# FFN1 of a hybrid transformer layer: a ring of three pairs of split weights for the down projections, single dots, another first loop

## The chip, the cores and the metric

The kernel runs on one core of a Trainium2 chip. The metric is the device time of one execution in microseconds; the time before is the median of three runs. Five engines work side by side, each through its own queue in order: TensorE (PE; its weight loads are listed as PEld), VectorE (DVE), ScalarE (ACT), GpSimd (POOL), and SyncE (SP), which here only issues transfers.

## The reference

One layer over 512 latent and 256 context tokens of width 1024: a half-step SwiGLU feed-forward network (FFN1), token mixing, and a second one. Each is modulated by nine vectors made from c (latent) and c_ctx (context). The change is in the modulation and in FFN1:

```python
mx = jnp.split((jax.nn.silu(c) @ w_ada + b_ada)[:, None, :], N_MOD, axis=-1)
mc = jnp.split((jax.nn.silu(c_ctx) @ w_ada + b_ada)[None, None, :], N_MOD, axis=-1)
x = ffn_sublayer(x, mx[0], mx[1], mx[2], norm1_w, ffn1_w1, ffn1_w3, ffn1_w2)
ctx = ffn_sublayer(ctx, mc[0], mc[1], mc[2], norm1_w, ffn1_w1, ffn1_w3, ffn1_w2)
...
def swiglu(h, w1, w3, w2):
    return (jax.nn.silu(h @ w1) * (h @ w3)) @ w2
def ffn_sublayer(h_in, shift, scale, gate, norm_w, w1, w3, w2):
    h = modulate(rms_norm(h_in, norm_w), shift, scale)
    return h_in + 0.5 * gate * swiglu(h, w1, w3, w2)
```

Here `modulate(h, shift, scale)` is `h * (1 + scale) + shift`. The inner width is 2816, that is 22 tiles of 128, named f = 0 to 21.

## The kernel before

All values lie with features on the partitions and tokens along the free axis, in the order of two groups A and B of 384 tokens (256 latent and 128 context each). To keep float32 precision with the fp32r matmul, every operand is split in two: a high part (`oph`, a cast on ScalarE, L103) and a low part (`opl`, a subtraction on VectorE, L104). Each product is then three matmuls: high by high (L131), high by low of the right side (L132), low by high (L133). The names in the trace follow: `hh`, `hl` are the halves of the modulated input, `gh`, `gl` those of the gated product, `opl` waits for `oph`.

**Weights.** `Stream.half` (L97) loads 128 x 1024 values into a ring of three buffers (`raw`), `Stream.block` (L89) loads 128 x 2048 into a ring of two (`block`). `operand` (L107) splits 512 columns into a ring of five pairs (`OPS`); up projections, down projections and the weights of later stages take turns in this ring.

**Modulation.** The products of silu(c) and silu(c_ctx) with `w_ada` are made in two ways. `ada_dot` (L225) is a dot on VectorE: a tile of 128 output features by 1024 inputs, times c broadcast over all partitions (`cb`), summed along the row. `ada_row` (L256) makes a row of 2 x 128 on TensorE by eight matmuls, copied by ScalarE, and `ada_col` (L264) turns it into a column by another matmul. In the first loop the scale comes by row, the shift by two dots (`ada_shift`, L270). The other seven vectors come by `ada_half` (L279): one load, and both dots (one from tile 40 on, where only latent tokens need them).

**Start.** Squares of x are made on ScalarE (`square0`), summed by seven adds on VectorE, and one matmul with ones (L423) sums over the partitions. Four warm-up matmuls (L415) stand ahead of it.

**First loop** (L465): over the eight input tiles k, with f = 0 and 1 accumulated in four banks (L462). Step k prepares the input of tile k+1 (`first_x` product, `first_h` shift and cast on ScalarE, `first_l` subtraction), then makes the twelve matmuls of tile k, then the row of tile k+2. The squares of the context are summed by GpSimd (L497) and the context's own matmuls (L455) run some steps later.

**Up projections.** f = 2 and 3 are plain (`up1`). From f = 4 each tile is a Strassen-Winograd pass of seven block products of twelve matmuls (`Winograd`: `head`, `mid`, `tail`), with four banks named X, Y, Z, W. Even tiles take them from the pool of single banks (`mm`), odd tiles from that of double banks (`big`). GpSimd makes the sums of weights (L592, L613 to L615), VectorE those of the results and the gating.

**Down projections.** They run in chunks of 3, 3, 4, 4, 3 and 5 tiles f (`CHUNKS1`), called by `after1` behind f = 5, 6, 10, 14 and 18, and the last after the loop. Each makes 16 sums (`pt`) in single banks, and VectorE adds them, gated, to x (L325).

**Order.** Start and first loop are kept in the order of the program. From L503 on a scheduler orders each engine's queue at build time. `Winograd.run` calls `step` three times per tile, each making one `ada_half`.

Of the kernel before, what the change touches and what calls it, by code (L numbers as in the profile page):

```python
# [16 lines left out]
P = 128  # L17
D = 1024
# [11 lines left out]
NFIRST = 2  # L30
W1 = 2 * NFIRST * P
# [4 lines left out]
WARM = 4  # L36
OPS = 5
GA, GB = (0, 384), (384, 384)
# [43 lines left out]
class Stream:  # L82
# [29 lines left out]
    def halves(self, src, eng=None):  # L112
        o = [self.operand(src[:, i : min(i + 512, src.shape[1])], eng) for i in (0, 512)]
        return Halves([t[0] for t in o]), Halves([t[1] for t in o])

    def unit(self, u, pool=None, tag=None):
        src = self.half(self.dram, u)
        if pool is None:
            return self.halves(src)
# [17 lines left out]
def layer_kernel(ctx: ExitStack, tc: tile.TileContext, xT, wfirst, wst, wada, wuq, wkpe, cols, wrope, vnw, rope, out):  # L137
# [31 lines left out]
    nhalf = const.tile([P, 8], F32, name="nhalf")  # L169

# [43 lines left out]
    units = [first_units(k) for k in range(2)]  # L214
# [41 lines left out]
    def ada_row(r, d):  # L256
        o = pa[0:2, (d % 2) * P : (d % 2) * P + P]
        for kt in range(NK):
            pin(nc.tensor.matmul(o, sc[:, kt, :], r[:, kt * P : kt * P + P], start=kt == 0, stop=kt == NK - 1))
        row = sp.tile([2, P], F32, tag="row", name=f"row_{d}")  # L260
# [3 lines left out]
    def ada_col(row, d):  # L264
        o = pa[:, 256 + 2 * d : 258 + 2 * d]
        pin(nc.tensor.matmul(o, row, ident[0:2, 0:2], start=True, stop=True))
        nc.vector.tensor_scalar(
            pairs[0][1][:, d, :], o, b1[:, NK + d : NK + d + 1], col[:, COL_N1 + d : COL_N1 + d + 1], ALU.add, ALU.mult)

    def ada_shift(r, d, alone=False):  # L270
        for which in range(2):
            ada_dot(r[:, D:], d, which, accs[:, d, which : which + 1])
            if alone:
                nc.vector.tensor_add(mod_s[0][which][:, d : d + 1], accs[:, d, which : which + 1], col[:, d : d + 1])
            yield
        if not alone:
            nc.vector.tensor_scalar_add(pairs[0][0][:, d, :], accs[:, d, :], col[:, d : d + 1])
# [91 lines left out]
    def square0(which, k):  # L369
# [1082 lines left out]
```

## Time and profile before

| | |
|---|---|
| median of three runs | 1205.05 us (1204.18 to 1205.37) |
| the profiled execution: time | 1204.45 us |
| its span, first to last instruction | 1202.7 us |
| its mean granted TensorE clock | 0.986 |
| TensorE busy | 1148.5 us (95%) |
| VectorE busy | 942.0 us (78%) |
| ScalarE busy | 537.1 us (45%) |
| GpSimd busy | 376.1 us (31%) |

The profile is of one execution. A row of the timeline has the start (us from the first instruction), the time of one group, the engine, the line, the operation, the tile written and those read, the shapes and the count; in brackets stands how long the engine was idle before it and what ended that. A line of the waits has the total in us, how often, and the longest. A window has its length, then busy time and count for each engine, the granted TensorE clock, the busy share of the 16 DMA engines and GB/s. L57 is the helper that keeps the start and the first loop in order, so rows there go by the tile's name. A matmul's own time is longer than the step from one to the next, since they overlap.

### The profile page before, as it was taken

The page shows a single profiled execution, that of the slowest core. Times are in us where ns is not written, and L with a number is a line of the kernel's source. Part 1 is how long each engine was busy: PE and PEld are TensorE (multiplying, and loading weights), DVE is VectorE, ACT ScalarE, POOL GpSimd, SP SyncE. Part 2 cuts the span into 40 slices and gives each one's busy share as a digit, 9 for nine tenths or more (in the row PEclk, how much of TensorE's full clock was granted, in tenths as well). Part 3 has the DMA queues.
Part 4 walks back from the last instruction along what each step waited for, and adds up shares of the span by engine and source line. Part 5 has one row for each costly group of instructions (what it writes and reads, how often), then busy time and mean ns, then how long its engine had stood idle before and what let it go on. Part 6 is the DMA issues. An engine that isn't in the chain of part 4 may idle for free. (4 is left out here: it accounts for less than half of the span.)

```text
span 1202.7 us, 18873 instructions
## 1 busy us (share of the span) xinstructions
PE 1148.5 (95%) x7066; PEld 1077.1 (90%) x7066; DVE 942.0 (78%) x1708; ACT 537.1 (45%) x1078; POOL 376.1 (31%) x336
## 2 busy tenths in 40 slices
PE   8899799979999999999999999999899999999998
PEld 6688699979999999999878878898898989899997
DVE  6999997896876877667973878775886878787884
ACT  5463222233144144244553537996553535353451
POOL 1201311222042033024333845784001424243330
PEclk9999999989999999999999999999999999999999
DMA  9444343243623633233322311101113332324212
GB/s 328 162 142 158 108 155 123 94 169 106 214 102 105 207 109 104 67 102 128 109 67 70 109 50 36 37 1 59 48 37 105 106 106 90 122 71 140 105 37 88
DMA packets 35228, 128.53 MB, mean 107 GB/s; under 512 B 3648, under 2 KB 10560, under 8 KB 29504
## 3 DMA queue, kind: packets, MB, share of 16 engines
q1 hardware_dynamic: 34992, 127.25, 31.6%
q8 instruction: 56, 0.92, 0.3%
q14 instruction: 36, 0.29, 0.1%
q10 hardware_dynamic: 144, 0.06, 0.0%
HBM read 125.20 MB, written 2.10 MB: 106 GB/s over the span
## 5 line engine op out<-in xcount | busy, mean ns | idle before, releaser
L103 ACT CAST oph<-block 128x512 fp32r<-128x512 f32 x216 | 134.0, 621 | 243.6 <-PE mm L132 163.9
L104 DVE TENSOR_TENSOR opl<-block,oph 128x512 fp32r<-128x512 f32 x216 | 192.5, 894 | 35.2 <-ACT oph L103 33.8
L131 PE MATMUL mm<-gh,oph 128*128 128x384 f32 (+2 forms) x532 | 187.3, 354 | 4.5 <-DVE x L325 3.9
L133 PE MATMUL mm<-gh,opl 128*128 128x384 f32 (+2 forms) x532 | 186.6, 354 | 4.5 <-DVE opl L104 4.5
L132 PE MATMUL mm<-gl,oph 128*128 128x384 f32 (+2 forms) x532 | 187.5, 352 | 0.0
L103 ACT CAST oph<-raw 128x512 fp32r<-128x512 f32 x140 | 85.5, 619 | 134.4 <-PE mm L132 74.9
L104 DVE TENSOR_TENSOR opl<-raw,oph 128x512 fp32r<-128x512 f32 x140 | 108.0, 778 | 21.6 <-ACT oph L103 21.1
L615 POOL TENSOR_TENSOR block<-block 128x512 f32<-128x512 f32 x35 | 47.2, 1348 | 242.2 <-DVE opl L104 214.5
L592 POOL TENSOR_TENSOR s<-block 128x512 f32<-128x512 f32 x35 | 52.2, 1493 | 216.8 <-DVE g L254 76.1
L131 PEld LDWEIGHTS mm<-gh,oph 128*128 128x128 f32 x532 | 100.1, 188 | 12.3 <-issue 4.3
L133 PEld LDWEIGHTS mm<-gh,opl 128*128 128x128 f32 x532 | 100.2, 188 | 12.0 <-DVE opl L104 5.4
L132 PEld LDWEIGHTS mm<-gl,oph 128*128 128x128 f32 x532 | 100.2, 188 | 6.6
L614 POOL TENSOR_TENSOR block<-s,block 128x512 f32<-128x512 f32 x35 | 51.3, 1467 | 166.7 <-DVE opl L104 165.0
L131 PE MATMUL big<-hh,oph 128*128 128x384 f32 (+1 forms) x240 | 80.1, 334 | 9.6 <-DVE gl L312 7.9
L325 DVE SCALAR_TENSOR_TENSOR x<-mm,g,x 128x256 f32<-128x256 f32 x194 | 71.1, 410 | 13.8 <-PE mm L133 13.7
L132 PE MATMUL big<-hl,oph 128*128 128x384 f32 (+1 forms) x240 | 80.0, 333 | 0.0
L133 PE MATMUL big<-hh,opl 128*128 128x384 f32 (+1 forms) x240 | 79.7, 332 | 0.0
L331 DVE SCALAR_TENSOR_TENSOR x<-mm,g,x 128x512 f32<-128x512 f32 x55 | 41.0, 748 | 48.7 <-PE mm L133 48.7
L229 DVE SCALAR_TENSOR_TENSOR junk<-raw,cb 128x1024 bf16<-128x1024 f32 x48 | 63.2, 1317 | 1.4 <-DMA raw<-wada 1.1
L132 PE MATMUL mm<-hl,oph 128*128 128x384 f32 x160 | 55.0, 344 | 2.5 <-DVE hl L308 2.5
L133 PE MATMUL mm<-hh,opl 128*128 128x384 f32 x160 | 54.4, 340 | 3.2 <-DVE opl L104 3.2
L131 PE MATMUL mm<-hh,oph 128*128 128x384 f32 x160 | 55.0, 343 | 1.1 <-DVE hh L307 0.7
(581 smaller groups left out, 3375.6 us busy)
## 6 DMA issues: line engine op xcount, KB each, us to landing
raw<-wst SPq DMA_DIRECT2D x82, 512.0 KB, 3.8
block<-wst SPq DMA_DIRECT2D x36, 1024.0 KB, 4.9
raw<-wada SPq DMA_DIRECT2D x56, 512.0 KB, 4.1
block<-wada SPq DMA_DIRECT2D x8, 1024.0 KB, 6.6
x<-xT SPq DMA_DIRECT2D x6, 512.0 KB, 6.7
raw<-wfirst SPq DMA_DIRECT2D x8, 256.0 KB, 5.1
out<-x SPq DMA_DIRECT2D x7, 256.0 KB, 2.5
raw<-wuq SPq DMA_DIRECT2D x2, 384.0 KB, 3.0
```

The source lines that it names most:

```text
L103: self.pin(self.nc.scalar.copy(dst[0], src))
L104: self.pin((eng or self.nc.vector).tensor_sub(dst[1], src, dst[0].bitcast(F32)))
L131: nc.tensor.matmul(out, lh, rh, start=first, stop=False, skip_group_check=more)
L132: nc.tensor.matmul(out, lh, rl, start=False, stop=False, skip_group_check=more)
L133: nc.tensor.matmul(out, ll, rh, start=False, stop=last, skip_group_check=more)
L229: nc.vector.scalar_tensor_tensor(out, raw, 1.0, cb[:, which, :], ALU.mult, ALU.mult, accum_out=acc[which][:, c : c + 1] if to is None else to,
L325: nc.vector.scalar_tensor_tensor(x[:, dt, s0 : s0 + sn], pt[:, o : o + sn], mod_g[i][which][:, dt : dt + 1], x[:, dt, s0 : s0 + sn], ALU.m ...
L331: nc.vector.scalar_tensor_tensor(lat(x, dt), two(pt), mod_g[i][0][:, dt : dt + 1], lat(x, dt), ALU.mult, ALU.add)
L592: (eng or nc.gpsimd).tensor_add(s1, q[2], q[3])
L614: eng.tensor_sub(q[0], s1, q[0])
L615: eng.tensor_sub(q[1], q[1], q[0])
```

## The change

FFN1's down projections split their weights into a ring of their own, three pairs in a new pool. In the Winograd passes the modulation is made dot by dot, in steps of 1, 2 and 1 a tile. Even tiles take the single banks in the order X, Y, W, Z. The first block is loaded in two transfers. The sum of squares at the start is four accumulated matmuls over pairs, with two of the squares made on VectorE; the warm-up matmuls go. For tiles 1, 2 and 3 the shift comes with the scale in a row of 256 on TensorE (`ROWS2`; the first blocks of `wada` are packed for it on the host). ScalarE takes over the small scale and shift operations, VectorE the context's squares from GpSimd. The row of tile k+2 now stands between the two halves of step k's matmuls, ahead of the preparation of tile k+1, and the context's part begins a step later.

```diff
+ROWS2 = (1, 2, 3)
-WARM = 4
+DOWNS = 3
...
-    def operand(self, src, eng=None):
-        o = [self.op_pool.tile([P, 512], F32R, tag=f"op{p}", bufs=self.op_bufs, name=f"op{p}_{self.nc.next_id()}") for p in "hl"]
+    def operand(self, src, eng=None, ring=None):
+        pool, tag, bufs = ring or (self.op_pool, "op", self.op_bufs)
+        o = [pool.tile([P, 512], F32R, tag=f"{tag}{p}", bufs=bufs, name=f"{tag}{p}_{self.nc.next_id()}") for p in "hl"]
...
-    units = [first_units(k) for k in range(2)]
+    u0, rw0 = st.raw_pool.tile([P, 2048], F32, tag="block", bufs=BLOCKS, name="block_first"), st.raw()
+    nc.sync.dma_start(u0[:, :D], wada[0][:, :D])
+    nc.sync.dma_start(u0[:, D:], wada[0][:, D:])
+    nc.sync.dma_start(rw0[:, :W1], wfirst[0])
+    units = [(u0, rw0), first_units(1)]
...
     def ada_row(r, d):
-        o = pa[0:2, (d % 2) * P : (d % 2) * P + P]
+        n = 2 * P if d in ROWS2 else P
+        o = pa[0:2, :n]
         for kt in range(NK):
-            pin(nc.tensor.matmul(o, sc[:, kt, :], r[:, kt * P : kt * P + P], start=kt == 0, stop=kt == NK - 1))
+            pin(nc.tensor.matmul(o, sc[:, kt, :], r[:, kt * n : kt * n + n], start=kt == 0, stop=kt == NK - 1))
...
     def ada_col(row, d):
-        o = pa[:, 256 + 2 * d : 258 + 2 * d]
-        pin(nc.tensor.matmul(o, row, ident[0:2, 0:2], start=True, stop=True))
-        nc.vector.tensor_scalar(
-            pairs[0][1][:, d, :], o, b1[:, NK + d : NK + d + 1], col[:, COL_N1 + d : COL_N1 + d + 1], ALU.add, ALU.mult)
+        o = [pcol[:, 4 * d + 2 * i : 4 * d + 2 * i + 2] for i in range(2)]
+        for i in range(2 if d in ROWS2 else 1):
+            pin(nc.tensor.matmul(o[i], row[:, i * P : i * P + P], ident[0:2, 0:2], start=True, stop=True))
+        nc.scalar.activation(
+            pairs[0][1][:, d, :], o[0], AF.Identity, bias=b1n[:, d : d + 1], scale=col[:, COL_N1 + d : COL_N1 + d + 1])
+        if d in ROWS2:
+            nc.scalar.activation(pairs[0][0][:, d, :], o[1], AF.Identity, bias=col[:, d : d + 1])
...
-    def ada_half(i):
-        r = st.half(wada, i)
-        for which in (0, 1) if i < 5 * NK else (0,):
-            ada_dot(r, i, which)
-            if i % NK == NK - 1:
-                mod_final(i // NK, slice(0, NK), which)
+    def ada_rest():
+        for i in range(2 * NK, 9 * NK):
+            r = st.half(wada, i)
+            for which in (0, 1) if i < 5 * NK else (0,):
+                ada_dot(r, i, which)
+                if i % NK == NK - 1:
+                    mod_final(i // NK, slice(0, NK), which)
+                yield
...
-    for i in range(WARM):
-        pin(nc.tensor.matmul(two(warm[:, :256]), ones, ones2, start=True, stop=True))
-    sa = None
-    for k in range(NK):
-        sa = add_sq(sa, k, square0(0, k), nc.vector)
+    for k in range(0, NK, 2):
+        sa = square0(0, k)
+        sb = square0(0, k + 1, k in (2, 6))
+        nc.vector.tensor_add(sa, sa, sb)
+        pin(nc.tensor.matmul(sumx, ones, sa, start=k == 0, stop=k == NK - 2))
...
-    ctx_h = {2: (0, 1), 3: (2, 3), 4: (4,), 5: (5,), 6: (6, 7)}
+    ctx_h = {3: (0, 1), 4: (2, 3), 5: (4, 5), 6: (6, 7)}
+    sqx = {0: 3, 1: 6, 2: 8}
...
+        for i in range(NFIRST):
+            first_mm(k, i)
+        if k + 1 < NK:
+            ada_col(row, k + 1)
+        if later:
+            o = ada_row(units[k + 2][0], k + 2)
+        for i in range(NFIRST, 2 * NFIRST):
+            first_mm(k, i)
         shift = ada_shift(units[k + 2][0], k + 2) if later else iter(())
+        next(shift, None)
         if k + 1 < NK:
             first_x(k + 1, 0)
             ops[k + 1] = st.operand(units[k + 1][1][:, :W1])
             first_h(k + 1, 0)
             next(shift, None)
             first_l(k + 1, 0)
+        if later:
+            row = ada_copy(o, k + 2)
...
-        if k == 0:
-            for j in range(NK):
-                sx = add_sq(sx, j, square0(1, j), nc.gpsimd)
+        if k in sqx:
+            while len(sqs) < sqx[k]:
+                sqs.append(square0(1, len(sqs)))
+                if len(sqs) > 1:
+                    nc.vector.tensor_add(sqs[0], sqs[0], sqs[-1])
...
-            banks = [bigs4[i] for i in (0, 2, 1, 3)] if f % 2 else [mm() for _ in range(4)]
+            mms = None if f % 2 else [mm() for _ in range(4)]
+            banks = [bigs4[i] for i in (0, 2, 1, 3)] if f % 2 else [mms[i] for i in (0, 1, 3, 2)]
...
     def after1(f):
         if f < NPLAIN1:
-            for _ in range(4):
-                ada_step()
+            ada_step(8)
         for ci, n in enumerate(CHUNKS1[:-1]):
             if f == (5 if ci == 0 else (starts1[ci] + n + 1) // 2 * 2):
-                down(starts1[ci], n, U_DN1 + starts1[ci], [GA, GB], lambda pt, dt, g, gn: evac_x(pt, dt, seg_of(g // 384), 0))
+                down(starts1[ci], n, U_DN1 + starts1[ci], [GA, GB], lambda pt, dt, g, gn: evac_x(pt, dt, seg_of(g // 384), 0),
+                     ring=(dnp, "dn", DOWNS))
...
+            dnp = fctx.enter_context(tc.tile_pool(name="ffn1d", bufs=DOWNS))
...
-    Winograd(gp, 384, U_UP1, blocks, g_tile, 1).run(NPLAIN1, after1, ada_step)
+    Winograd(gp, 384, U_UP1, blocks, g_tile, 1).run(NPLAIN1, after1, lambda f, i: ada_step(1 + (i == 1)))
```

More of the change, by code (lines that the diff above doesn't have):

```diff
@@ L435, in layer_kernel @@
     first_l(0, 0)
+    row = ada_copy(ada_row(units[1][0], 1), 1)
     put_cb(1)
@@ L438, in layer_kernel @@
         pass
-    row = ada_row(units[1][0], 1)
-    for _ in ada_shift(units[1][0], 1):
-        pass
-    ada_col(row, 1)
     pbs = bigs(4)
     pcs = []
-    sx = None
     def first_ctx(k):
@@ L482, in layer_kernel @@
             first_h(j, 1)
-        for i in range(2 * NFIRST):
-            first_mm(k, i)
-        if later:
-            row = ada_row(units[k + 2][0], k + 2)
-        next(shift, None)
         for j in ctx_h.get(k, ()):
@@ L491, in layer_kernel @@
             first_ctx(j)
-        next(shift, None)
-        if later:
-            ada_col(row, k + 2)
-        if k == 0:
-            for j in range(NK):
-                sx = add_sq(sx, j, square0(1, j), nc.gpsimd)
-        if k == 1:
+        if k in sqx:
[3 more added lines that the diff above has]
+                    nc.vector.tensor_add(sqs[0], sqs[0], sqs[-1])
+        if k == 2:
             sumx = mm()[:, :256]
-            pin(nc.tensor.matmul(sumx, ones, sx, start=True, stop=True))
+            pin(nc.tensor.matmul(sumx, ones, sqs[0], start=True, stop=True))
         if k == 5:
```

78 lines of the change are left out of this document (41 added, 37 removed).

## The prediction

> **What bounds the kernel now.** I read the page first (busy shares), then the waits of TensorE in the first half, then the busy times by stage, then the timeline at each long wait.
>
> ```profile
> PE 1148.5 (95%) x7066; PEld 1077.1 (90%) x7066; DVE 942.0 (78%) x1708; ACT 537.1 (45%) x1078; POOL 376.1 (31%) x336
> ```
>
> TensorE is busy 1148.5 of 1202.7 us. So a gain can only come from its 54 us of idle time, or from time at a lowered clock. The waits of TensorE up to 620 us (total, times, longest) say what the idle time is:
>
> ```profile
> PE mm L133 <- DVE opl L104: 9.3, 5, 3.2
> PE big L131 <- DVE gl L312: 7.9, 1, 7.9
> PE mm L500 <- POOL sq L57: 3.9, 1, 3.9
> PE big L131 <- DVE sl L319: 1.1, 2, 0.9
> PE big L131 <- ACT p L605: 0.6, 1, 0.6
> PE mm L131 <- ACT oph L103: 0.6, 1, 0.6
> PE big L131 <- ACT oph L103: 0.6, 1, 0.6
> ```
>
> The long ones are waits for VectorE, and one for GpSimd. The stages (us; busy time and count of PE, weight loads, DVE, ACT, POOL; granted clock; DMA share; GB/s):
>
> ```profile
> 0.00:20.49 20.49, 16.27 (x85) 12.54 (x85) 11.44 (x23) 13.11 (x22) 0.68 (x6) 1.00 0.97 325
> 20.49:78.03 57.54, 50.18 (x292) 38.78 (x292) 54.38 (x107) 31.22 (x68) 8.88 (x7) 0.97 0.57 196
> 78.03:150.86 72.83, 62.19 (x349) 59.44 (x350) 71.56 (x114) 25.04 (x50) 17.66 (x11) 0.99 0.38 125
> 150.86:156.11 5.25, 5.25 (x16) 5.25 (x17) 5.25 (x10) 0.96 (x2) 0.00 (x0) 0.50 0.91 357
> 248.00:262.00 14.00, 6.11 (x22) 5.79 (x21) 14.00 (x26) 3.32 (x7) 4.12 (x3) 0.63 0.63 228
> 262.00:484.00 222.00, 222.00 (x1280) 221.68 (x1278) 172.22 (x308) 75.54 (x141) 55.58 (x39) 1.00 0.41 136
> ```
>
> From 20 to 151 us VectorE is busy 126 of 130 us and TensorE waits 18 us: this stretch is bound by VectorE. The same holds at 248 us for one long wait. From 262 to 484 us TensorE never waits; there nothing can be won. The stages after FFN1 are not touched.
>
> **Part 1: the start (0 to 20.49 us).** The squares of x were summed on VectorE in one chain of seven adds, then one matmul. Now two squares are made on VectorE, pairs are added (six operations), and four matmuls accumulate.
>
> ```profile
> 7.13 5.47 DVE L57 TENSOR_TENSOR sq<-sq,sq 128x512 f32<-128x512 f32 x7 [2.68 <-ACT sq L57]
> 10.48 1.89 PE L415 MATMUL mm<-ones 128*128 128x256 f32 x8
> 12.66 1.12 PE L423 MATMUL mm<-sq,ones 128*128 128x512 f32 x2 [0.29 <-DVE sq L57]
> 20.18 0.38 PE L266 MATMUL mm<-ident,row 2*128 2x2 f32 x2 [1.34 <-ACT row L57]
> 20.49 0.50 PE L462 MATMUL big<-hh,oph 128*128 128x512 f32 x1
> ```
>
> Seven dependent adds took 5.47 us, 0.78 each; six that wait less take about 0.72 each, 4.3. So the last add ends 1.2 us earlier, and the three earlier matmuls lie under it. The first main matmul then waited at 20.18 for a row copied on ScalarE behind the second big copy of c (L436); in the new order that copy comes after the row's. Against it stands the doubled row of tile 1 (+1.7, below). The first block now comes in two transfers, one more issue on SP's queue ahead of block 1 and of the context's x; the queues behind it are full at this time, so it costs nothing beyond the place in the queue. I take 1.8 us gained, between 0.5 and 2.5.
>
> The four warm-up matmuls of L415 leave. The Trainium skill (TensorE: Matmul & The Clock Gate, Part 1) says that the array falls to half clock after an idle window of about 3.4 us, which speaks against taking them out: the first 3.4 us of work would then cost 1.7 us more. Without them the gap would be 10.5 to 12.7, 2.2 us, and the earlier matmuls of the squares lie in it; by the trace I expect no loss, by the rule at its worst 1.7 us.
>
> **Part 2: the first loop (20.49 to 78.03 us).** Work leaves VectorE:
>
> ```profile
> L57 DVE SCALAR_TENSOR_TENSOR junk<-block,cb 128x1024 bf16<-128x1024 f32 x15 | 19.3, 1289 | 0.2 <-ACT cb L57 0.2
> L57 DVE TENSOR_TENSOR hl<-hfull,hh 128x256 fp32r<-128x256 f32 x7 | 2.8, 419 | 0.0
> L57 DVE TENSOR_SCALAR s<-accs,col 128x2 f32<-128x2 f32 x7 | 2.3, 325 | 0.1
> L57 DVE TENSOR_SCALAR a<-mm,b,col 128x2 f32<-128x2 f32 x7 | 1.9, 275 | 2.4 <-PE mm L266 2.4
> 27.23 9.35 POOL L57 TENSOR_TENSOR sq<-sq,sq 128x256 f32<-128x256 f32 x7 [25.95 <-ACT sq L57]
> 26.62 0.69 DVE L57 TENSOR_TENSOR hl<-hfull,hh 128x512 fp32r<-128x512 f32 x1
> 33.15 1.20 DVE L57 TENSOR_TENSOR hl<-hfull,hh 128x512 fp32r<-128x512 f32 x1
> ```
>
> Six dots go (tiles 1 to 3 get their shift from TensorE): 6 x 1.14 (start to start, rows in part 4) = 6.8. The small scale and shift operations go to ScalarE (31 of 57.5 us busy): 2.3 + 1.9 = 4.2. GpSimd's seven adds go; while they ran (9.35 us) the same VectorE subtraction took 1.20 instead of 0.69, so about 3 us more. Seven adds of 256 columns come, at 0.42: 2.9. Net 11 us off 54.4: VectorE needs 43 us and is no longer the bound.
>
> TensorE becomes it. Its rows of the modulation cost:
>
> ```profile
> 20.49:78.03 57.54, 11.45 (x96) 7.65 (x96) 18.89 (x30) 0.00 (x0) 0.00 (x0) 0.97 0.57 196
> ```
>
> Six rows in 11.45 us, 1.91 each, with 128 columns. Three are now 256 wide. The doubling costs between nothing (fixed cost) and 1.9; the 16 records follow each other at about 0.11 us, so it is the columns that count, and I take 1.7. Two of the three lie in this loop: +3.4, and +0.5 for three more column matmuls. TensorE's work at full clock is 50.18 less 1.7 (half of the 3.4 us at half clock that 0.97 of 57.54 makes) = 48.5, so 52.4 now. To this I add 2 us for two waits that I see in the new order: tile 2's row now stands in the middle of step 0, and its block comes over queues that are 97% busy at 325 GB/s (x of 768 columns, 3.1 MB, three blocks of 1.05 and two first weights of 0.26 are 6.8 MB: 21 us, against 20 when TensorE asks); and the sum of the context's squares ends on VectorE just as TensorE wants it. So 54.5 against 57.54: 3 us, between -2 and 5.
>
> A wait is added: VectorE's product with x (L390) now waits for ScalarE's scale, and behind it in VectorE's queue stand the split of the weights and the subtraction hl, for which TensorE's next step waits. From the column matmul it is ScalarE, VectorE, twice ScalarE, VectorE, some 0.7 each as hl above and 0.3 for the first: 3.1 us. TensorE has the next tile's row (1.9 or 3.6) and half a step of products (six at 0.23) in that time, 3.3 or more, and the context's products from step 4: covered, but with little to spare in step 3, which is why my lower bound is below zero.
>
> **Part 3: up to the first down projection (78.03 to 156 us).** TensorE idles 72.83 - 62.19 = 10.6 us, and its last wait costs clock as well:
>
> ```profile
> 150.86 0.69 PE L133 MATMUL mm<-gh,opl 128*128 128x384 f32 x1 [3.18 <-DVE opl L104]
> 151.35 0.52 PE L131 MATMUL mm<-gh,oph 128*128 128x384 f32 x1
> 151.67 0.52 PE L132 MATMUL mm<-gl,oph 128*128 128x384 f32 x1
> 156.81 0.33 PE L132 MATMUL mm<-gl,oph 128*128 128x384 f32 x1
> 156.98 0.33 PE L133 MATMUL mm<-gh,opl 128*128 128x384 f32 x1
> ```
>
> Matmuls start 0.32 us apart until 156.1 and 0.17 after: 5.25 us at half clock, 2.6 lost. Up to the tile f=5 the built program now has 24 dots after the first loop where there were 35, since dots come one by one instead of in pairs: 11 x 1.14 = 12.5 us off VectorE's 71.6, so 59 against TensorE's 62.2, and it arrives with a lead from the loop as well. The waits that are not backlog (ScalarE's copies and the gating product, 1.1 + 0.6 + 0.6 + 0.6) stay: 2.9. Gain 10.6 - 2.9 + 2.6 = 10.3, between 5 and 13. The ring itself (down weights no longer take turns with the up weights' five buffers) is in this term: the wait at 150.86 is for a down weight. At each turn of the new ring ScalarE waits for TensorE to let go of a pair, as it does now.
>
> **Part 4: the long wait (248 to 262 us).**
>
> ```profile
> 242.48 1.28 DVE L104 TENSOR_TENSOR opl<-block,oph 128x512 fp32r<-128x512 f32 x2
> 243.69 1.21 DVE L229 SCALAR_TENSOR_TENSOR junk<-raw,cb 128x1024 bf16<-128x1024 f32 x1
> 244.83 2.31 DVE L229 SCALAR_TENSOR_TENSOR raw<-raw,cb 128x1024 f32<-128x1024 f32 x1
> 249.28 0.56 DVE L637 TENSOR_TENSOR big<-big,u 128x384 f32<-128x384 f32 x1
> 249.75 0.55 DVE L634 TENSOR_TENSOR big<-big,sl 128x384 f32<-128x384 f32 x1
> 256.46 0.69 PE L131 MATMUL big<-hh,oph 128*128 128x384 f32 x1 [7.89 <-DVE gl L312]
> 261.42 0.53 PE L131 MATMUL mm<-u4h,oph 128*128 128x384 f32 x1
> 262.16 0.34 PE L131 MATMUL mm<-u4h,oph 128*128 128x384 f32 x1
> ```
>
> By start to start a dot costs 1.14 us (beside GpSimd up to 2.3), a split 0.6, a 384-wide operation 0.47. The pass up to f=8 held 8 dots: 8 x 1.14 + 8 x 0.6 + 8 x 0.47 = 17.7, and more beside GpSimd, against 84 matmuls x 0.173 = 14.5 on TensorE. Now the passes f=8 to 10 hold 4, 4 and 3 dots: 4.6 + 4.2 + 3.8 = 12.6, about 15 with GpSimd. The backlog that made the wait (7.9, and matmuls of 0.53 instead of 0.34 from 256.5 to 261.7 behind it, 2.6 us) grows by half a microsecond a pass instead of 3 to 6. Gain 9.5, between 4 and 10.5. The new bank order (W before Z in even tiles) helps the same release and is not counted again.
>
> **Part 5: the rest.** The dots go somewhere: the down projections behind f=10 and f=14 hold 15 where there were 12, which is 3.4 us of VectorE in stretches of 48 us of TensorE, hidden while VectorE (172 of 222 us) has room. A dot that waits for its load has the evacuations of x behind it, and those free the four banks of the down projection. I charge 1 us, from 0 to 6, and 1 us more for the new turns of the ring.
>
> **The sum.** The profiled execution took 1204.45 us (span 1202.7, and 1.75 around it); the median of the runs is 1205.05, so no correction. 1.8 + 3 + 10.3 + 9.5 - 2 = 22.6: 1204.45 - 22.6 = 1182.
>
> **Rivals.** *The loop gives nothing*: TensorE's 5 us of wider rows and their waits for blocks eat what VectorE gives up. For it: queues at 97%. Against: from block 3 on a step of 6 us needs 1.3 MB, 4 us at 325 GB/s. Parts 3 to 5 alone: 1187.
>
> *A wait comes back later*: VectorE falls behind in a pass that held no dots before (f=12, 16, 17), or behind a late load, once for as long as the wait at 248: 7.9 + 2.6. For it: every dot moved is moved to a later place. Against: 50 us of room from 262 to 484. 1193.
>
> *The change doesn't do what it says*: the backlog is of splits and GpSimd's slowing rather than dots, so parts 3 and 4 give a third: 1182 + 13 = 1195.
>
> *Slower*: ScalarE stands at the cast of a down pair until TensorE lets go of one of only three, and behind it wait the casts of the next up products. 22 units in two pairs are 44 turns. For it: casts already held TensorE 0.6 us at a time. From 0.55 us a turn it eats the 24.6 us that the other parts bring, at 0.7 with two falls to half clock (5 us) the time is 1204.45 + 11 = 1216. Against: five shared buffers made just one long wait in a down projection so far.
>
> **How the numbers follow.** Forecast 0.55; loop nothing 0.17; wait back 0.12; backlog of splits 0.07; slower 0.09. The forecast's own range is 1176 to 1190. The range is 1174 (all parts at their upper bounds, less a little) to 1198 (the third rival with a small loss). Faster than 0.2% (2.4 us, about what a measurement can tell from no change): the first three and most of the fourth, 0.87; same 0.04; slower 0.09.
>
> **What would show it.** The first main matmul near 18.7 us; the wait on GpSimd's squares gone; VectorE near 43 us busy in the first loop; no 3.18 and 7.89 waits and no half clock at 151 and 256; the product that waited until 150.86 near 138. I am wrong if a wait of over 3 us stands anywhere from 80 to 480 us, or if ScalarE's waits for TensorE at down weights stop TensorE.

## The result, and the profile after

The changed kernel is slower by 0.55%: 1208.48 us (median of 7) against 1202.33 of the kernel before on the same chip, ratio 1.0055 [1.0039, 1.0071]. The profiled execution has a span of 1205.1 us against 1202.7, so the two profiles lie closer together than the medians. First the busy times of its page, then TensorE's waits up to 620 us (total, times, longest):

```profile
PE 1151.6 (96%) x7070; PEld 1072.5 (89%) x7070; DVE 931.9 (77%) x1686; ACT 539.5 (45%) x1093; POOL 365.8 (30%) x329
```

```profile
PE big L133 <- DVE u L638: 17.7, 4, 7.3
PE mm L133 <- DVE hh L324: 1.8, 2, 1.1
PE big L472 <- DVE hl L58: 1.8, 2, 1.1
PE mm L135 <- DVE opl L105: 1.8, 3, 1.1
```

The waits of 7.9, 9.3 and 3.9 us (for `gl`, `opl` and GpSimd's `sq`) are gone. In their place stands one kind that the kernel before did not have: 17.7 us for the Y sum, the addition of bank Y and the copied first product (`u`, L638). The windows by stage (busy time and count for PE, weight loads, DVE, ACT, POOL; granted clock; DMA share; GB/s):

```profile
0.00:18.73 18.73, 16.64 (x81) 9.63 (x81) 10.09 (x20) 10.97 (x19) 0.68 (x6) 1.00 0.97 319
18.73:78.33 59.60, 53.47 (x300) 38.21 (x300) 45.38 (x87) 36.82 (x85) 0.00 (x0) 1.00 0.55 201
78.33:150.35 72.02, 63.25 (x357) 61.01 (x357) 71.40 (x114) 26.32 (x53) 17.34 (x11) 1.00 0.41 133
248.00:262.00 14.00, 12.20 (x69) 11.57 (x68) 14.00 (x22) 6.75 (x13) 4.99 (x3) 1.00 0.31 88
324.00:339.00 15.00, 7.67 (x37) 7.35 (x36) 10.86 (x23) 3.38 (x6) 1.60 (x2) 0.77 0.80 287
425.00:438.00 13.00, 7.37 (x27) 7.06 (x26) 11.46 (x22) 2.86 (x5) 1.94 (x2) 0.74 0.89 310
```

The first window ends with the first main matmul, the second with the first plain product (78.03 before). In the stretch at 248 us TensorE is busy 12.20 of 14 us now (6.11 before); the holes are at 332 and 431, at the ends of the down projections behind f=10 and f=14. From TensorE's timeline:

```profile
150.35 0.44 PE L133 MATMUL big<-u3h,oph 128*128 128x384 f32 x1 [3.98 <-DVE u L638]
332.20 0.69 PE L133 MATMUL big<-u3h,oph 128*128 128x384 f32 x1 [7.33 <-DVE u L638]
...
431.54 0.69 PE L133 MATMUL big<-u3h,oph 128*128 128x384 f32 x1 [5.63 <-DVE u L638]
```

A mark along the way is the start of the Y sum of each tile on VectorE (after minus before, us; negative is earlier):

| f | 5 | 6 | 7 | 8 | 9 | 10 | 11 | 14 | 15 | 16 | 17 | 21 |
|---|---|---|---|---|---|---|---|---|---|---|---|---|
| after | -0.98 | -2.57 | -4.29 | -11.01 | -11.07 | -9.64 | -3.12 | -2.19 | +5.18 | +7.49 | +8.89 | +7.44 |

So 11 us are won up to f=9 and 18.5 lost from there to f=21, in two steps of 6.5 and 7.4 us, each with a down projection in it, and smaller ones. What stands in VectorE's queue at the first of them, the changed kernel first, then the kernel before:

```profile
328.70 1.23 DVE L236 SCALAR_TENSOR_TENSOR raw<-raw,cb 128x1024 f32<-128x1024 f32 x1 [0.92 <-DMA raw<-wada]
329.85 0.08 DVE L236 DVE_READ_ACCUMULATOR raw<-raw,cb 128x1 f32 x1
329.85 0.69 DVE L105 TENSOR_TENSOR opl<-block,oph 128x512 fp32r<-128x512 f32 x1
330.45 1.22 DVE L236 SCALAR_TENSOR_TENSOR raw<-raw,cb 128x1024 f32<-128x1024 f32 x1
331.60 0.08 DVE L236 DVE_READ_ACCUMULATOR raw<-raw,cb 128x1 f32 x1
331.60 0.55 DVE L638 TENSOR_TENSOR u<-big,p 128x384 f32<-128x384 f32 x1
```

```profile
329.14 1.22 DVE L229 SCALAR_TENSOR_TENSOR raw<-raw,cb 128x1024 f32<-128x1024 f32 x1
...
331.62 1.39 DVE L325 SCALAR_TENSOR_TENSOR x<-mm,g,x 128x256 f32<-128x256 f32 x4
332.92 1.89 DVE L104 TENSOR_TENSOR opl<-block,oph 128x512 fp32r<-128x512 f32 x3
334.72 0.55 DVE L620 TENSOR_TENSOR u<-big,p 128x384 f32<-128x384 f32 x1
```

After, the last dots stand behind the last x additions and directly ahead of the Y sum, each paced by its load, and TensorE's W product, in the same double bank as Y, waits 7.33 us. Before, the last dot ended at 330.4 with x additions and splits still to come, and TensorE never waited. The loads and casts show what has changed ahead of the dots (SyncE's and ScalarE's timelines and the first product of the down projection; after, then before):

```profile
276.33 0.44 PE L133 MATMUL mm<-gh,dnh 128*128 128x384 f32 x1 [0.33 <-ACT sl L635]
306.01 0.62 ACT L104 CAST dnh<-raw 128x512 fp32r<-128x512 f32 x1 [3.53 <-PE mm L134]
289.66 37.74 SPq L100 DMA_DIRECT2D raw<-wada  x14
331.70 6.77 SPq L100 DMA_DIRECT2D raw<-wst  x3
336.17 1.14 ACT L104 CAST dnh<-raw 128x512 fp32r<-128x512 f32 x2 [3.46 <-DMA raw<-wst]
```

```profile
290.24 0.34 PE L131 MATMUL mm<-gh,oph 128*128 128x384 f32 x1
307.00 0.62 ACT L103 CAST oph<-raw 128x512 fp32r<-128x512 f32 x1 [3.55 <-PE mm L132]
295.87 28.99 SPq L99 DMA_DIRECT2D raw<-wada  x12
```

A down weight keeps its load buffer until its second half is cast. With three pairs the last such cast comes 29.7 us after the first product, with five it came at 16.8; meanwhile the dots have fewer of the three buffers. (Some products run ahead in the changed kernel. Counted back from the last product, at 318.30 and 328.08, the cast is 12.3 and 21.1 us away: 9 us later, not 13.) And the pairs that fall free at the end are taken at once by the next chunk: its casts (336.17) stand in ScalarE's queue 41 us ahead of that chunk's first product (377.54), and wait for loads that SyncE issues behind the dots' (331.70).

### The profile page after: what moved, and what is told of

It reads as the page before. It is cut to its first block, busy times and chain, and to the rows that moved or that the text cites. A ratio compares the mean times of both kernels' runs of the same rounds, so it can differ in the third digit from the quotient of the medians.

```text
span 1205.1 us, 18833 instructions
## 1 busy us (share of the span) xinstructions
PE 1151.6 (96%) x7070; PEld 1072.5 (89%) x7070; DVE 931.9 (77%) x1686; ACT 539.5 (45%) x1093; POOL 365.8 (30%) x329
## 5 line engine op out<-in xcount | busy, mean ns | idle before, releaser
L133 PE MATMUL mm<-gh,dnh 128*128 128x384 f32 x352 | 118.1, 336 | 0.6 <-ACT sl L635 0.3
L134 PE MATMUL mm<-gl,dnh 128*128 128x384 f32 x352 | 117.8, 335 | 0.0
L135 PE MATMUL mm<-gh,dnl 128*128 128x384 f32 x352 | 116.9, 335 | 0.8 <-DVE dnl L105 0.7
L104 ACT CAST oph<-raw 128x512 fp32r<-128x512 f32 x86 | 52.4, 620 | 58.9 <-PE mm L134 31.4
L105 DVE TENSOR_TENSOR opl<-raw,oph 128x512 fp32r<-128x512 f32 x86 | 64.2, 754 | 10.9 <-ACT oph L104 10.7
L134 PE MATMUL mm<-gl,oph 128*128 128x512 f32 (+1 forms) x180 | 69.3, 385 | 0.0
L135 PE MATMUL mm<-gh,opl 128*128 128x512 f32 (+1 forms) x180 | 69.1, 385 | 0.0
L133 PE MATMUL mm<-gh,oph 128*128 128x512 f32 (+1 forms) x180 | 68.8, 385 | 0.0
L133 PEld LDWEIGHTS mm<-gh,dnh 128*128 128x128 f32 x352 | 66.2, 188 | 1.8 <-ACT dnh L104 1.0
L135 PEld LDWEIGHTS mm<-gh,dnl 128*128 128x128 f32 x352 | 66.0, 188 | 1.5 <-DVE dnl L105 1.5
```

The lines of the kernel that those rows point to most:

```text
L104: self.pin(self.nc.scalar.copy(dst[0], src))
L105: self.pin((eng or self.nc.vector).tensor_sub(dst[1], src, dst[0].bitcast(F32)))
L133: nc.tensor.matmul(out, lh, rh, start=first, stop=False, skip_group_check=more)
L134: nc.tensor.matmul(out, lh, rl, start=False, stop=False, skip_group_check=more)
L135: nc.tensor.matmul(out, ll, rh, start=False, stop=last, skip_group_check=more)
```

## The experiments

Eighteen kernels; "before" is the kernel before in the same session. The last column names the expectation (given below, ahead of each result) in whose range the time lies.

| run | kernel | us | ratio to before | in the range of |
|---|---|---|---|---|
| e1 | changed, dots in pairs | 1219.01 | 1.0144 [1.0123, 1.0164] | B |
| e2 | changed, no ring | 1199.58 | 0.9984 [0.9972, 0.9996] | none, between A and B |
| e3 | before, with the new start and first loop | 1201.12 | 0.9987 [0.9976, 0.9998] | none, nearest to "gives nothing" |
| e4 | changed, five dots a tile to f=9, then three | 1223.11 | 1.0169 [1.0147, 1.0190] | B |
| e5 | e1, next chunk's loads held | 1206.48 | 1.0032 [1.0016, 1.0048] | none, 2.5 above O |
| e6 | changed, next chunk's loads held | 1208.77 | 1.0055 [1.0037, 1.0074] | T |
| e7 | changed, eight pairs in one ring | 1203.08 | 1.0010 [0.9996, 1.0024] | none, between O and M |
| e8 | no ring, two load buffers for the dots | 1214.16 | 1.0107 [1.0073, 1.0142] | the rival |
| e9 | no ring, dots held | 1216.67 | 1.0101 [1.0079, 1.0123] | G |
| e10 | changed, dots held | 1207.64 | 1.0046 [1.0027, 1.0065] | O |
| e11 | changed, ring of two pairs | 1213.24 | 1.0076 [1.0052, 1.0100] | D |
| e12 | changed, dots and loads held | 1209.55 | 1.0056 [1.0038, 1.0073] | D |
| e13 | no ring, three lots of 12 dots | 1207.11 | 1.0023 [1.0012, 1.0034] | none |
| e14 | no ring, lots of 13 and 14 | 1202.75 | 0.9998 [0.9984, 1.0011] | W |
| e15 | ring, three lots of 12 between the sums | 1197.37 | 0.9935 [0.9918, 0.9952] | none, 0.6 below D |
| e16 | e15, lots behind the sums | 1210.71 | 1.0063 [1.0041, 1.0085] | none, 0.7 above P |
| e17 | e15, lots two sums later | 1193.87 | 0.9908 [0.9884, 0.9933] | none, 0.1 below P |
| e18 | e15, next chunk's loads held | 1203.92 | 1.0008 [0.9990, 1.0026] | none |

**One part at a time (e1 to e4).** Theory A: the dots in the down projections are too many and their loads late. Theory B: the ring does it. e1, dots in pairs:

```diff
-                yield
+            yield
...
-            ada_step(8)
+            ada_step(4)
...
-lambda f, i: ada_step(1 + (i == 1))
+lambda f, i: ada_step()
```

> The changed kernel with one part undone: the modulation dots in pairs again, three loads a tile as before (12 dots behind f=10 and f=14 instead of 15 to 16). Theory A (too many loaded dots behind a down projection's end): the waits of 7.3 us at 332 and 5.6 us at 431 and the half clock behind both go, about 20 us; the passes up to f=9 hold 8 dots again, so up to 10.5 us come back near 248: between 1190 and 1199 us. Theory B (the ring of three pairs makes those waits): they stay, and the time is 1208 or above.

e2, no ring (both calls of `down`):

```diff
-            dnp = fctx.enter_context(tc.tile_pool(name="ffn1d", bufs=DOWNS))
...
-                     ring=(dnp, "dn", DOWNS))
```

> The changed kernel without the second ring: down weights share the five pairs again, dots stay single. Theory A: 13 and 16 dots stand behind f=10 and f=14, 3 and 2 of them behind the last addition to x, so waits of 3 to 6 us stay near 330 and 430: 1203 to 1210 us. Theory B: both waits go and the time falls by 15 us or more, to 1193 or less.

e3 has the edits of e1 and e2, and the old order of banks:

```diff
-            mms = None if f % 2 else [mm() for _ in range(4)]
-            banks = [bigs4[i] for i in (0, 2, 1, 3)] if f % 2 else [mms[i] for i in (0, 1, 3, 2)]
+            banks = [bigs4[i] for i in (0, 2, 1, 3)] if f % 2 else [mm() for _ in range(4)]
```

> The kernel before with the new start and first loop alone (dots in pairs, no second ring, old bank order). If the loop is worth what was forecast, 1197 us (5 less than before). If it gives nothing, because TensorE's wider rows eat VectorE's relief (first plain product at 78.3 us against 78.0), within 1 us of before, with the waits at 151 and 248 as they were.

e4, another pace of the dots:

```diff
-lambda f, i: ada_step(1 + (i == 1))
+lambda f, i: ada_step((2 if i else 1) if f < 10 else 1)
```

> The changed kernel with another pace of the dots: five a tile up to f=9, three a tile from f=10, so that 12 dots stand behind f=10 and f=14 as before. Theory A: neither the waits at 332 and 431 nor the long one at 248 (5 dots a pass instead of 8): 1186 to 1194 us, below both kernels. Theory B: the waits at 332 and 431 stay, 1203 us or more.

The ring costs 8.9 us with single dots (1208.48 against e2, from two sessions) and 17.9 with pairs (e1 against e3, which also differ in the banks). The loop and the start give 1.3 us. In e1 the long wait is still there (7.91 us, at 255.51), so the new order of banks does not remove it; the single dots do. In e2 the waits near 330 and 430 fall to 2.77 us or less, but its Y sum, 12.3 us ahead of the kernel before at f=9, is only 1.9 ahead at f=21: the single dots lose 10.4 us there without any ring (e3, with pairs, loses nothing there). In e4 12 dots stand in each of the two down projections, as before, and it is the slowest of all: A falls as a theory of the count. In e1 and e4 the long waits behind the two down projections are not at the Y sum but at a cast (6.07 and 3.78 us; 5.77 and 5.73 us). ScalarE's and TensorE's timelines of e1 show how:

```profile
337.19 1.14 ACT L104 CAST dnh<-raw 128x512 fp32r<-128x512 f32 x2 [7.48 <-DMA raw<-wst]
338.23 0.61 ACT L104 CAST oph<-block 128x512 fp32r<-128x512 f32 x1
...
341.39 0.61 ACT L104 CAST oph<-block 128x512 fp32r<-128x512 f32 x1
```

```profile
341.54 0.69 PE L133 MATMUL mm<-hh,oph 128*128 128x384 f32 x1 [6.07 <-ACT oph L104]
```

The casts of the chunk behind f=14 wait 7.48 us for their loads, the casts of tile f=11 wait behind them, and TensorE behind those.

**The next chunk's casts, and the memory (e5 to e8).** e5 (on e1) and e6 (on the changed kernel) tie the loads of a chunk's first two units to its last gated product, by a copy of one column:

```diff
-    def half(self, src, i):
+    def half(self, src, i, late=None):
         t = self.raw()
+        if late is not None:
+            self.nc.gpsimd.tensor_copy(t[:, :1], late)
...
-                        us[q] = st.unit(u0 + q, ring=ring)
+                        us[q] = st.unit(u0 + q, ring=ring, late=gt[f0 + n - 1][0][:, :1].bitcast(F32) if ring and cache is None and q in (0, 1) else None)
```

> Changed kernel with dots in pairs (as in the run that took 1219.01), ring kept, but the loads of a chunk's first two down units are held until the chunk's last gated product exists (a one-column GpSimd copy into the load's buffer). Theory O (order): the ring's cost is that its pairs are free as soon as a down projection ends, so the casts of the NEXT chunk are put there, ahead of the casts of the up pass that follows, and stand in ScalarE's queue for late loads (7.48 us at 337 in that run). Then this run has no wait over 3 us at the up product behind f=10 and f=14, and takes 1199 to 1204. Rival T (turns): three pairs are too few, a cast stands until TensorE lets go of one. The turns are the same here, so 1214 to 1221.

> The changed kernel itself with the same hold. Theory O: the casts of the next chunk leave the passes f=11 and f=15, and the time falls to that of the kernel without the ring (1199.6), 1196 to 1201; of the waits of 7.33 and 5.63 us at the Y sum behind f=10 and f=14 at most 3 us each stay, since 15 dots paced by loads are still there. Rival T: as the changed kernel, 1206 to 1210.

e7, the same pairs in one ring, and e8, the memory for load buffers instead:

```diff
+        self.turn = (self.turn + 1) % (self.op_bufs + DOWNS)
+        ring = self.more if self.turn < DOWNS else None
```

```diff
-            r = st.half(wada, i)
+            r = adp.tile([P, 1024], F32, tag="adaraw", bufs=DOWNS, name=f"adaraw_{i}")
+            nc.sync.dma_start(r, wada[i // 2][:, (i % 2) * 1024 : (i % 2) * 1024 + 1024])
```

> The changed kernel with the same eight pairs in one ring, in which up and down weights take turns. Theory O: turns in program order keep the next chunk's casts out of the pass that follows, so 1195 to 1201 although the memory is the same. Rival M (any more pairs let the splits run ahead of the sums and dots on VectorE, whichever ring): no better than the changed kernel, 1206 or more.

> No second ring; the dots' loads get two buffers of their own instead (8 KB a partition where the ring took 12). Theory O says further that what singles gain up to f=9 (12.3 us in the run without the ring) is given back where 13 to 16 dots paced by loads through three shared buffers stand in a down projection. Here 10 and 8 are there, and 5 to 6 in each of the passes between, so the 12.3 us are kept: 1188 to 1193. Rival: five to six dots a pass are more than VectorE has room for (6 x 1.14 + 7 x 0.6 + 8 x 0.47 = 14.8 us against 14.5 of TensorE) and the wait moves there: 1198 or more.

With pairs the hold gives back 12.5 of 17.9 us, and no wait over 3 us is left behind f=10 and f=14: there the early casts are the larger part of the ring's cost. In the changed kernel it gives nothing (e6: 5.67 and 5.49 us of waits at the Y sum remain, behind dots). So the early casts are not its bound; the time is in T's range, but the waits end with VectorE's Y sum and not with a cast, so T's reason is not shown by it. e7 lies between the two bounds. e8 missed by over 20 us: with buffers of their own the dots run ahead to where VectorE has no room. The Y sum of f=4 comes 9.7 us later than before, and from f=11 to f=14, with five or six dots a pass, another 15 us go.

**The dots held (e9 to e12).** From f=11 each dot's load is tied in the same way to the gated product of the tile before, so that 4 to 8 stand in a down projection; e9 without the ring, e10 with it, e12 with the hold of e6 as well. e11 changes `DOWNS` alone.

```diff
-            r = st.half(wada, i)
+            r = st.half(wada, i, late[0])
...
+    def paced(f, i):
+        late[0] = gt[f - 1][0][:, :1].bitcast(F32) if f >= 11 else None
+        ada_step(1 + (i == 1))
```

```diff
-DOWNS = 3
+DOWNS = 2
```

> No second ring, and from f=11 the load of a dot waits for the gated product of the tile before (a one-column GpSimd copy into its buffer), so that dots cannot be pulled into a down projection: 4, 8 and 8 stand behind f=10, 14, 18 instead of 13, 16 and 4, and 3 to 5 in the passes between. Theory D (crowding): the 12.3 us that single dots gain up to f=9 were given back because 13 to 16 loads of 2.4 us each through three shared buffers do not fit into a down projection of 39 us, and VectorE works in order. Then 1188 to 1193, faster than both kernels. Rival G: the extra GpSimd copies, or dots in passes that had none, cost as much: 1197 or more.

> The changed kernel with its ring, dots held in the same way (4, 5 and 4 behind f=10, 14, 18). Theory D: with three pairs a down weight sits in its load buffer until its last half is cast, 27.5 us into the down projection instead of 16.8, so the dots' loads start late, and the last dot ends 48 to 51 us after the start instead of 40. That hurts through the dots alone, so here the ring costs little: no wait over 3 us from 280 to 450, 1189 to 1196. Rival O (the casts of the next chunk, put ahead of the next pass, do the harm by themselves): 1200 or more.

> The changed kernel with a ring of two pairs instead of three. Theory D: the last cast of a down unit comes one turn of 4.15 us later still (30 us or more into the down projection), the last dot too, so 1209 to 1218. Rival O (casts of the next chunk put ahead): one pair less can be put ahead, so less harm: 1200 to 1206.

> The changed kernel with its ring, and both the dots' loads (as in the run before last) and the first two down loads of a chunk held. Theory D: as the run with held dots and ring, within 3 us of it, since without crowded dots the early casts find their loads in time. Rival O: at least 5 us better than that run.

In e10 the wait behind f=10 is gone (Y sum of f=11 at -11.3 us against before, -3.1 in the changed kernel): dots at the end of a down projection are what TensorE waited for. But the gain is lost again: by f=14 it is -3.3, for eight dots in the passes f=13 and 14. So e10 missed D, and its time lies in the range of Rival O; but e12, which takes the early casts away as well, is no better than e10, which speaks against O. e11 did what D said (last cast 33.0 us after the first product, waits of 5.26 and 5.96 us). e9 missed D by over 20 us. Two things follow: fewer pairs do not help (e11's interval overlaps that of the changed kernel, so that they make it worse is not shown), and from f=11 on the dots have no cheap place in the passes.

**The dots dealt out between the sums (e13 to e18).** Four dots a tile up to f=10, then one behind each of the first twelve of a down projection's 16 sums, held as in e9. e13 is without the ring, e15 with it; e14 is e13 with thirteen and no dots at f=10.

```diff
+    def evac_dot(pt, dt, g, gn):
+        evac_x(pt, dt, seg_of(g // 384), 0)
+        if left[0] > 0 and (2 * dt + (g > 0)) >= 0 and (2 * dt + (g > 0)) % 1 == 0:
+            left[0] -= 1
+            ada_step()
...
+        if f in (10, 14, 18):
+            left[0], late[0] = 12, gt[f - 1][0][:, :1].bitcast(F32)
```

> No second ring; single dots, four a tile up to f=10 as in the change, and the rest in three lots of 12 dealt out between the sums of the down projections behind f=10, 14 and 18 (each load waits for the gated product of the tile before), none in the passes between. Theory D: twelve loads of 2.4 us fit into a down projection (the kernel before does it, last dot 40 us after the start), so the 10 to 12 us that singles gain up to f=10 are kept to the end: 1189 to 1194. Rival W (VectorE's whole work up to f=21 sets the pace, wherever the dots stand): 1198 to 1203, as without the ring.

> The same with no dots at f=10 and 13, 13 and 14 in the three lots. Theory D: the wait behind f=9 (2.1 to 2.3 us for a cast at 260 in the runs without the ring) shrinks, the last dot of a lot ends 2.4 us later, about 42 us after the start of the down projection and still before the next Y sum at 44: within 2 us of the run before, 1188 to 1195. Rival W: 1198 to 1203.

> The changed kernel with its ring and the same three lots of 12. Theory D: the down weights sit in the load buffers until 27.5 us into the down projection instead of 16.8, so the last dots end some 8 us later than in the run without the ring, at 46 to 48 us, past the next Y sum, and the ring costs 3 to 6 us at each of three places: 1198 to 1208. Rival N (the ring is harmless once the lots are right): within 3 us of the run with twelve and no ring.

e16 puts the lots behind the sums, e17 lets them begin two sums later, e18 adds the hold of e6 to e15:

```diff
-            ada_step()
...
+                ada_step(left[0])
+                left[0] = 0
```

```diff
-        if left[0] > 0 and (2 * dt + (g > 0)) >= 0 and (2 * dt + (g > 0)) % 1 == 0:
+        if left[0] > 0 and (2 * dt + (g > 0)) >= 2 and (2 * dt + (g > 0)) % 1 == 0:
```

> As the run with twelve and the ring (1197.37), with one difference: the lots of 12 are put behind the sums of their down projection in the program instead of between them; the built order still has 12 dots in each of the three. Theory P (place): what the ring costs comes from where the dots stand among the sums. Behind the sums they come last, their loads behind the down weights' that sit in the load buffers until the ring's third pair is free, and the next Y sum waits behind them, as in the changed kernel: 1203 to 1210, with a wait of over 2 us at the Y sum behind f=10 or f=14. Rival C (count: 12 fit, 15 do not, wherever they stand): 1195 to 1200.

> As the run with twelve and the ring, but the lots begin two sums later. Theory P: still between the sums and done before the last of them, so 1194 to 1201. Rival: the early start was what helped (the loads come ahead of the down weights'), 1202 or more.

> As the run with twelve and the ring, with the first two down loads of a chunk held as well (as in the run with pairs, where that gave back 12.5 us). Theory P: the casts of the next chunk find their loads in time when dots do not crowd the end of the down projection, so nothing is won: 1195 to 1200. Rival O (the early casts cost by themselves): 1193 or less.

e15 contradicted what I had concluded: with the ring and the dots between the sums the kernel is 0.65% faster than before, without the ring (e13) it is slower. e16 settles what the place is worth with the ring. It has three lots of 12 dots like e15, the ring like e15, and only their place in the program differs: 1210.71 against 1197.37. The wait at the Y sum that P expected behind f=10 or f=14 is not there; TensorE waits for a cast, 5.31 and 4.33 us, and the queues look like those of e1 (SyncE, ScalarE, TensorE):

```profile
322.02 7.33 SPq L102 DMA_DIRECT2D raw<-wst  x4
326.97 1.14 ACT L106 CAST dnh<-raw 128x512 fp32r<-128x512 f32 x2 [19.79 <-DMA raw<-wst]
330.39 0.69 PE L135 MATMUL mm<-hh,oph 128*128 128x384 f32 x1 [5.31 <-ACT oph L106]
```

In e17 the last dot of the lot ends ahead of the additions of the last seven sums, VectorE waits for TensorE there and not the other way, and TensorE's longest waits up to 620 us are 2.7 us, at 151, and 1.7:

```profile
315.80 1.23 DVE L238 SCALAR_TENSOR_TENSOR raw<-raw,cb 128x1024 f32<-128x1024 f32 x1 [0.90 <-DMA raw<-wada]
...
324.36 0.74 DVE L346 SCALAR_TENSOR_TENSOR x<-mm,g,x 128x256 f32<-128x256 f32 x2 [1.31 <-PE mm L137]
325.02 0.55 DVE L642 TENSOR_TENSOR u<-big,p 128x384 f32<-128x384 f32 x1
```

```profile
PE mm L135 <- DVE x L346: 3.7, 6, 1.2
PE big L135 <- DVE u L642: 3.7, 2, 2.7
```

The gain at the Y sums is -9.3 us at f=14, -8.3 at f=18 and -5.2 at f=21. e17 is the fastest of all, faster than both kernels; its interval overlaps that of e15, so that it beats e15 is not shown. e18 missed both theories: the hold, which won 12.5 us in e5, loses 6.5 here.

## Why the prediction was wrong, by its own steps

The terms of the sum, cut at the first main matmul, the first plain product, and the Y sums of f=6, 9 and 21 (us gained in the profiled executions):

| term | forecast | measured |
|---|---|---|
| start | +1.8 | +1.76 (20.49 to 18.73) |
| first loop | +3 | -2.06 (57.54 to 59.60) |
| to the first down projection (f=6) | +10.3 | +2.87 |
| long wait (f=6 to f=9) | +9.5 | +8.50 |
| rest of the passes (f=9 to f=21) | -2 | -18.51 |
| behind FFN1's passes | 0 | +5.04 |

*Part 1 was right*, and the clock is 1.00 there without the warm-up matmuls. The 1.7 us that the rule of the Trainium skill (TensorE: Matmul & The Clock Gate, Part 1) would have cost at its worst did not come due.

*Part 2: the mechanism was right, its worth was not.* VectorE fell to 45.38 us (forecast 43), TensorE's work is 53.47 (52.4), GpSimd's wait is gone. What failed is "to this I add 2 us for two waits". The two came to 2.2 us (1.02 for the block at 21.96, 1.18 for the squares at 40.73), but five more, up to 1.10 for `hl` at 71.78, make 6.0 in all. The loop is a chain from engine to engine; time taken off VectorE became its own idle time. The forecast named such a chain and held it to be covered. e3 gives 1.3 us for start and loop together. The rival "the loop gives nothing" was right here.

*Part 3 rested on a miscount.* "24 dots where there were 35": the trace of the kernel before has 26. The nine too many match nine small sums (`s<-accs,col`, from 13.9 to 66.2 us) that read the dots' results; seven of them are in the row x7 of part 2. Grouped by line, changed kernel and kernel before, from the first plain product to the wait at 150 us:

```profile
L236 DVE SCALAR_TENSOR_TENSOR junk<-raw,cb 128x1024 bf16<-128x1024 f32 x24 | 32.1, 1339 | 0.4 <-DMA raw<-wada 0.2
```

```profile
L229 DVE SCALAR_TENSOR_TENSOR junk<-raw,cb 128x1024 bf16<-128x1024 f32 x26 | 34.8, 1338 | 0.5 <-DMA raw<-wada 0.3
```

Two dots left, 2.7 us, and three more splits of weights stand ahead of the Y sum of f=5 (24 against 21, together 2.1 us longer; three of the 24 fill the new ring). VectorE is busy 71.40 of 72.02 us there, as full as before. Nor was there a lead from the loop to arrive with. On the down weight the step was right: the product that had waited until 150.86 is the third of the down projection, and it now starts 8.1 us earlier (forecast near 138):

```profile
142.78 0.34 PE L135 MATMUL mm<-gh,dnl 128*128 128x384 f32 x1
```

But the wait came back behind it: 3.98 us at 150.35, for the Y sum of f=5, which is only 0.98 us earlier than before.

*Part 4 was right*: 8.5 us against 9.5, and the window at 248 shows clock 1.00 and no long wait. e1 against the changed kernel, which differ in the dots alone, shows that it is the single dots.

*Part 5 is where the sign turned.* "I charge 1 us, from 0 to 6, and 1 us more for the new turns of the ring" became 18.5 us. By e2's profile, which loses 10.4 us in the same stretch without a ring, a good half of it is the dots in their new places and about 8 us the ring. The sentence before it named the right queue, but followed the dots only to the additions of x; behind those stands the Y sum, for which TensorE's W product waits. It also took the 12 dots of the kernel before as the measure for 15, where what hid them was their place between the sums. And the ring was costed by its turns (3.53 us of waiting at a cast, as before), not by what a longer wait for a pair keeps occupied (load buffers, 9 to 13 us longer) nor by what a free pair invites (the next chunk's casts).

*The slower rival* had the right sign and not the mechanism. Casts wait for TensorE to let go of a pair no longer than before, and no wait of TensorE begins there. What ScalarE stands at, in e1, is a load of a chunk that is not needed yet. "A wait comes back later" was nearest: two waits, 7.33 and 5.63 us, both at places with late loads; it was priced at one. (Of the chances, 0.87 for faster holds 0.03 of the fourth's 0.07, which is not most of it.)

The +5 us behind the passes stay open. About 3.3 of them are clock: from 600 to 625 and from 625 to 650 us it is 1.00 and 0.93 in the changed kernel, 0.94 and 0.86 before. In the twenty profiles the time behind the Y sum of f=21 runs from 656.2 to 662.5 us, and the longest is that of the kernel before. The medians differ by 6.15 us where the two profiles differ by 2.4, so most of this gain seems to belong to the two executions and not to the change; that is not shown.

**What is shown, and what stays open.** Shown: the ring costs 9 to 18 us as the change has it and gains with the dots dealt out (e15 against e13, one session, 9.7 us); with the ring, the place of the dots among the sums decides (e16 against e15); with pairs, the next chunk's early casts are most of the ring's cost (e5 against e1). Read from traces only: that the load buffers, held longer, make the dots late; e11 agrees, but an extra load buffer beside the three pairs was not tried. Open: whether it is the dots' place on VectorE or that of their loads (in e16 SyncE issues ten loads of dots in a row and then four of weights, in e15 they alternate; the two move together), why the lots gain nothing without the ring (e13 and e14 wait 2 to 5 us for x additions and `gl` inside the down projections), why the hold loses in e18, and whether a better place than that of e17 exists.

## What to carry to other kernels

Filler work that waits for its own loads is safer ahead of the last work that frees a bank (13 us between e15 and e16), and what follows in that engine's queue beyond it must be followed until an engine on the path appears; the number of fillers alone says little (12 in e4, e15 and e16). A new ring is costed by what it lets start early and by what is kept occupied upstream while its fewer slots turn, not by its turns alone, since the scheduler of this kernel fills a free slot at once and puts the work ahead of what is due. Count operations in a trace by a grouped row, with name and shape, before building a term of ten microseconds on them.

## What the runs showed of the hardware

The half clock behind a long wait does not grow with the wait. At half clock matmuls start 0.32 us apart instead of 0.17. In the changed kernel waits of 3.98, 7.33 and 5.63 us were followed by 3.5, 3.1 and 6.1 us of it (windows as above; the third lasts until 437.6):

```profile
150.35:153.80 3.45, 3.45 (x12) 3.45 (x13) 3.45 (x8) 0.90 (x2) 0.00 (x0) 0.59 0.76 273
332.20:335.30 3.10, 3.10 (x10) 3.10 (x11) 2.29 (x4) 0.48 (x1) 0.66 (x1) 0.50 0.98 330
431.54:437.60 6.06, 6.06 (x19) 6.06 (x20) 5.46 (x9) 2.24 (x4) 1.54 (x2) 0.50 0.95 352
```

In the kernel before 3.18 and 7.89 us were followed by 5.25 and 5.3. So such a wait cost itself and 1.5 to 3 us more. After the 3.98 us the first three matmuls still went at full speed (150.35, 150.63, 150.80) and the slow ones began at 150.98: the clock can fall behind the hole, not in it. A shorter wait can cost as much: in e9 one of 2.99 us ended at 148.18, and 5.8 us at half clock followed; in e2 one of 2.32 us ended at 259.95, and 3.05 us followed; in e11 one of 3.38 us ended at 150.21, and none followed (e9 twice, e2, e11):

```profile
148.18:151.50 3.32, 3.32 (x10) 3.32 (x11) 2.70 (x6) 1.71 (x4) 0.00 (x0) 0.50 0.82 259
151.50:154.00 2.50, 2.50 (x9) 2.50 (x9) 0.94 (x2) 0.62 (x1) 0.00 (x0) 0.50 0.89 300
259.95:263.00 3.05, 3.05 (x10) 3.05 (x10) 1.64 (x3) 0.85 (x2) 1.27 (x1) 0.50 0.80 282
150.20:153.50 3.30, 3.29 (x19) 3.29 (x19) 2.72 (x7) 1.52 (x3) 0.00 (x0) 1.00 0.85 313
```

The Trainium skill (TensorE: Matmul & The Clock Gate, Part 1) has a window of about 3.4 us that runs freely, with one idle window to lower the clock and one busy window to raise it. The stretches of 3.05 to 3.5 us are near to that window, and the late fall fits one that runs freely. Those of 5.25 to 6.1 us are longer than one such window, and the waits of 2.32 and 2.99 us that were followed by half clock are shorter, and there the measurement decides.
